# Sparse attention in a four-layer decoder trunk: the compressed branch by four heads of a token tile, its values on 128 rows, and the last queries projected ahead of the last values

## The chip, the core and the metric

The kernel runs on one core of one Trainium2 chip. The core has five engines that take their instructions in order: TensorE (PE in the profile; PEld is its weight load), VectorE (DVE), ScalarE (ACT), GpSimd (POOL) and SyncE (SP), which issues most DMAs. The metric is the device time of one execution in microseconds (us).

## What is computed

A trunk of four layers over 256 tokens of width 1024, all in float32. Each layer is a pre-RMSNorm token mixer and a squared-ReLU MLP of width 4096. The mixers are native sparse attention (layer 0), stick-breaking attention, a Conformer convolution and block-sparse attention. The change touches the mixer of layer 0 only:

```python
q = _apply_rope(_rms_norm(q), cos, sin)                 # 8 heads of 128
kc, ks, kw = [rope(rms_norm(k))]                        # 2 groups, 4 heads each
kc = einsum('bnlgd,lde->bnge', kc[:, cidx] + pos, w_cmp[0])   # blocks of 32, stride 16
vc = einsum('bnlgd,lde->bnge', vc[:, cidx] + pos, w_cmp[1])
p_c = _masked_softmax(q . kc * scale, cmp_end <= t);  o_c = p_c @ vc
p_s = _masked_softmax(q . k_selected * scale, causal); o_s = p_s @ v_selected
p_w = _masked_softmax(q . kw * scale, window);        o_w = p_w @ vw
o = gate0 * o_c + gate1 * o_s + gate2 * o_w
out = o.reshape(B, S, H * DH) @ w_out
```

With 256 tokens there are four selection blocks and the top 16 are taken, so the selected branch sees every block, and the window of 512 sees every token: both are plain causal attention with their own keys and values. The compressed branch has 15 blocks in each of the two groups, 30 rows, held as 32.

## The kernel before

Activations are held feature-major, in 8 tiles of 128 features by 256 tokens, and tokens in two tiles of 128. A float32 weight is split into a high and a low part in the type fp32r (`piece`, L142: ScalarE casts the high part at L159, VectorE subtracts at L160), and a projection does three fp32r matmuls in place of one (`mm3`, L181 to L186). Attention itself works in plain float32; one such matmul appears in the trace as two records.

`nsa` (L424) is layer 0. `chunk(ci)` (L484) projects one chunk of the input weights for both token tiles, in the order of `NSA_CHUNKS`: compressed keys and values; selected and window keys; queries of heads 0 to 3; values of group 0 with the gates; values of group 1 with the query of head 4; queries of heads 5 to 7. `queries` (L468) takes the norm of a head (sum of squares, then a power on GpSimd, L385), its negated copy `nrq` (L471) and the rope on VectorE (L392, L393, L402). `transpose_to` (L455) queues four transposes and their copy in the list `waiting`, which `flush` or the next projection empties.

`compress(kv)` (L542) forms the block sums: 64 matmuls of 32 columns (L553) from two DMAs of 1 MB, a copy `part` (L559), and one matmul with 0/1 entries (`quarters`) that adds the parts: for keys it gives 32 columns, copied behind the 256 keys in `kcat`; for values 32 rows, `vcmp`.

`scores(h, t)` (L569) is one head and token tile (a unit): the masks are added by matmuls of the identity with the mask (L579, L581, L594, L597), then the query meets the keys of the selected, window and compressed branch (L583 for the first tile, L599 and L604 for the second). VectorE takes three maxima and the negative scaled maximum `nm` (L611), ScalarE three exponentials with their sums (L615), VectorE the reciprocals times the gates (L618 to L620) and the scaling (L622, L623). `mix(h, t, pr)` (L627) transposes the probabilities on TensorE (L633; the 32 compressed columns at L637), copies them, and multiplies by the values (L642; the compressed ones at L643 with 32 rows). `attend` runs a list of units with the mix one unit behind the scores: first the four heads of group 0, later `UNITS` for group 1. `Out` (L231) is the output projection `wo`: 192 matmuls of 256 columns (L212 to L214, tile `acc`).

A scheduler of the framework sets the order of the instructions on each engine when the program is built. It may move work of a later call ahead, so output-projection and query-projection matmuls stand between the steps of attention. PSUM tiles rotate in tags A (2 banks), B (4) and C (2); the names `sc`, `pt`, `pc` are in B, `pp` and `po` in C.

Of the kernel before, what the change touches and what calls it, by code (L numbers as in the profile page):

```python
# [16 lines left out]
P = 128  # L17
# [50 lines left out]
def trunk(ctx: ExitStack, tc: tile.TileContext, A: dict, out: bass.AP):  # L68
# [355 lines left out]
    def nsa(n, first):  # L424
        aT = n.xT
        nxt = start_norm(4)
        with tc.tile_pool(name="nsa", bufs=1) as sp:
# [12 lines left out]
            vcmp = sp.tile([32, DH], F32, name="vcmp")  # L440
            quarters = sp.tile([P, 32], F32, name="quarters")
            oT = act.tile([P, KT, 2, NT, P], F32R, tag="aT", name="oT")
            with tc.tile_pool(name="nsw", bufs=2) as wp:
# [40 lines left out]
                def chunk(ci):  # L484
# [10 lines left out]
                    for t in range(NT):  # L495
# [24 lines left out]
                        elif ci == 5:  # L520
                            queries(t, o[:, :384], 5, 3)
                        else:
                            g = ci - 3
# [6 lines left out]
                            else:  # L530
                                queries(t, o[:, 256:384], 4, 1)
# [10 lines left out]
                def compress(kv):  # L542
# [13 lines left out]
                    if kv == 0:  # L556
                        flush()
# [3 lines left out]
                    if kv == 0:  # L561
                        nc.tensor.matmul(pt[:, :32], lhsT=part, rhs=quarters, start=True, stop=True)
                        for g in range(2):
                            nc.scalar.copy(kcat[:, g, 256:288], pt[:, :32])
                    else:
                        nc.tensor.matmul(pt[:32, :DH], lhsT=quarters, rhs=part, start=True, stop=True)
                        nc.scalar.copy(vcmp, pt[:32, :DH])

                def scores(h, t):  # L569

# [4 lines left out]
                    mx = sm.tile([P, 3], F32, tag="mx", name="mx")  # L575
                    if t == 0:

                        s0 = bank("B", "sc")
                        nc.tensor.matmul(s0[:, 256:288], lhsT=identr, rhs=mk[:, P + 32 * g:][:, :32],  # L579
                                         start=True, stop=False, skip_group_check=True)  # L580
                        nc.tensor.matmul(s0[:, :256], lhsT=identr, rhs=diag2, start=False, stop=False,  # L581
                                         skip_group_check=True)
                        nc.tensor.matmul(s0[:, :288], lhsT=q, rhs=kcat[:, g, :288], start=False, stop=True,  # L583
                                         skip_group_check=True)
                        nc.vector.tensor_reduce(mx[:, 0:2], s0[:, :256].rearrange("p (a b) -> p a b", b=P),
                                                axis=AX.X, op=ALU.max)
                        views = [s0[:, :P], s0[:, P:256], s0[:, 256:288]]
                    else:

                        kb = kcat[:, g]  # L590
                        views = []
                        for br in range(2):
                            s0 = bank("B", f"sc{br}")
                            nc.tensor.matmul(s0[:, P:256], lhsT=identr, rhs=mk[:, :P], start=True, stop=False,  # L594
                                             skip_group_check=True)
                            if br == 0:
                                nc.tensor.matmul(s0[:, 256:288], lhsT=identr, rhs=mk[:, P + 64 + 32 * g:][:, :32],  # L597
                                                 start=False, stop=False, skip_group_check=True)
                                nc.tensor.matmul(s0[:, 256:288], lhsT=q, rhs=kb[:, 256:288], start=False, stop=False,  # L599
                                                 skip_group_check=True)  # L600
                                cmp_view = s0[:, 256:288]
                            rhs = bass.AP(tensor=kb.tensor, offset=kb.offset + br * P,
                                          ap=[kb.ap[0], [288, 2], [1, P]])
                            nc.tensor.matmul(s0[:, :256], lhsT=q, rhs=rhs, start=False, stop=True,  # L604
                                             skip_group_check=True)
                            nc.vector.tensor_reduce(mx[:, br:br + 1], s0[:, :256], axis=AX.X, op=ALU.max)
# [587 lines left out]
```

## Time and profile before

| | us |
|---|---|
| median of 3 runs | 1199.9 (1198.47 to 1200.67) |
| profiled execution, whole | 1198.12 |
| profiled execution, span from the first to the last instruction | 1196.3 |
| TensorE busy in the span | 1174.8 (98%) |
| VectorE, ScalarE, GpSimd busy | 779.8, 623.4, 34.7 |
| layer 0's mixer, from the first matmul to the first of the MLP | 7.6 to 147.2 |

TensorE is busy nearly all the time. Its records overlap, because a matmul starts before the one ahead of it has ended, so a busy time is not what a matmul adds. The chain of waits gives each piece from the end of the one before it, and so what it adds.

### The profile page before, as it was taken

What the parts mean: (1) busy time and instruction counts of PE and PEld (TensorE: products, weight loads), DVE (VectorE), ACT (ScalarE), POOL (GpSimd) and SP (SyncE); (2) the same over time, 40 slices, a digit from 0 to 9 for tenths busy, and PEclk for the clock granted to TensorE, in tenths of its full rate; (3) what the DMA queues carried; (4) which work ended last, traced back from release to release, by engine and by line L of the source; (5) the groups of instructions that cost most, each with busy time, mean ns of one, the idle gap of its engine ahead of it and who ended that gap; (6) DMA issues with size and microseconds to landing.
All of it is one profiled execution on the core that took longest, in us unless ns stands there. A gap on an engine that the chain in (4) does not pass through costs nothing.

```text
span 1196.3 us, 17644 instructions
## 1 busy us (share of the span) xinstructions
PE 1174.8 (98%) x7042; PEld 1010.6 (84%) x7042; DVE 779.8 (65%) x1203; ACT 623.4 (52%) x1027; POOL 34.7 (3%) x46
## 2 busy tenths in 40 slices
PE   7999999999999999999999899999999999999998
PEld 5888988888888898888889898888888789888886
DVE  7678676556585477566665578556558876666553
ACT  6477554544465655444553276444447665544441
POOL 1200000000000000000001000000001010000000
PEclk9999999999999999999999999999999999999999
DMA  8553164554454425554546826455354633555440
GB/s 310 189 183 142 71 212 160 196 207 167 185 188 163 154 91 205 207 211 161 196 159 203 257 107 239 148 211 206 146 202 158 222 116 110 208 203 188 172 176 36
DMA packets 35073, 211.23 MB, mean 177 GB/s; under 512 B 4528, under 2 KB 7472, under 8 KB 11440
## 3 DMA queue, kind: packets, MB, share of 16 engines
q1 hardware_dynamic: 30816, 200.99, 46.8%
q0 software_dynamic: 1280, 4.70, 1.4%
q10 hardware_dynamic: 2896, 4.42, 1.1%
q8 instruction: 55, 0.90, 0.3%
q14 instruction: 26, 0.21, 0.1%
HBM read 207.87 MB, written 2.23 MB: 176 GB/s over the span
## 4 chain that ended last, share of the span: by engine, by line
PE 66%; issue 26%; DVE 4%; DMA 2%; ACT 1%; POOL 1%; SPq 0%; ACTq 0%; DVEq 0%; POOLq 0%
PE projT L205 22%; PE dn L186 7%; PE dn L184 7%; PE dn L185 7%; PE ab L873 2%; PE proj L184 2%; PE proj L186 2%; PE proj L185 2%; PE acc L212 2%; PE acc L213 2%; PE acc L214 2%; DVE wl L160 1%; PE po L642 1%; ACT wh L159 1%; PE cv L817 1%
## 5 line engine op out<-in xcount | busy, mean ns | idle before, releaser
L160 DVE TENSOR_TENSOR wl<-raw,wh 128x1024 fp32r<-128x1024 f32 (+2 forms) x376 | 446.0, 1210 | 190.0 <-ACT wh L159 185.3
L159 ACT CAST wh<-raw 128x1024 fp32r<-128x1024 f32 (+2 forms) x376 | 379.7, 1040 | 207.8 <-PE dn L186 111.2
L205 PE MATMUL projT<-xT,wh 128*128 128x512 f32 x1152 | 361.6, 396 | 0.3 <-DVE xT L101 0.3
L205 PEld LDWEIGHTS projT<-xT,wl 128*128 128x128 f32 x1152 | 215.3, 188 | 49.7
L205 PE MATMUL projT<-xT,wl 128*128 128x256 f32 x1152 | 225.8, 278 | 0.0
L184 PE MATMUL dn<-wh,u 128*128 128x512 f32 x512 | 202.7, 396 | 0.0
L186 PE MATMUL dn<-wh,u 128*128 128x512 f32 x512 | 202.0, 395 | 0.0
L185 PE MATMUL dn<-wl,u 128*128 128x512 f32 x512 | 201.4, 393 | 0.0
L205 PEld LDWEIGHTS projT<-xT,wh 128*128 128x128 f32 x1152 | 178.3, 189 | 3.5 <-DVE xT L101 0.5
L186 PEld LDWEIGHTS dn<-wh,u 128*128 128x128 f32 x512 | 96.4, 188 | 22.3
L185 PEld LDWEIGHTS dn<-wl,u 128*128 128x128 f32 x512 | 96.4, 188 | 20.9
L184 PEld LDWEIGHTS dn<-wh,u 128*128 128x128 f32 x512 | 96.5, 188 | 20.3
L184 PE MATMUL proj<-wh,xT 128*128 128x512 f32 (+2 forms) x224 | 87.0, 390 | 8.0 <-ACT wh L159 7.6
L310 ACT COPY b<-projT 128x256 f32<-128x256 f32 x128 | 41.2, 374 | 93.8 <-PE projT L205 93.4
L185 PE MATMUL proj<-wl,xT 128*128 128x512 f32 (+2 forms) x224 | 85.9, 384 | 0.0
L186 PE MATMUL proj<-wh,xT 128*128 128x512 f32 (+2 forms) x224 | 85.7, 383 | 0.0
L311 DVE TENSOR_TENSOR s<-projT,b 128x256 f32<-128x256 f32 x128 | 48.1, 417 | 55.0 <-ACT b L310 55.0
L89 ACT CAST u<-q 128x1024 fp32r<-128x1024 f32 x32 | 33.6, 1049 | 82.8 <-DVE q L313 82.7
L212 PE MATMUL acc<-oT,wh 128*128 128x256 f32 x256 | 73.6, 292 | 0.1
L213 PE MATMUL acc<-oT,wh 128*128 128x256 f32 x256 | 72.9, 286 | 0.0
L214 PE MATMUL acc<-oT,wl 128*128 128x256 f32 x256 | 71.0, 284 | 0.0
L90 DVE TENSOR_TENSOR u<-q,u 128x1024 fp32r<-128x1024 f32 x32 | 39.2, 1226 | 34.6 <-ACT u L89 34.6
(251 smaller groups left out, 1243.5 us busy)
## 6 DMA issues: line engine op xcount, KB each, us to landing
raw<-in_up SPq DMA_DIRECT2D x64, 1024.0 KB, 4.8
raw<-in_down SPq DMA_DIRECT2D x64, 1024.0 KB, 4.9
raw<-in_sb_w SPq DMA_DIRECT2D x12, 1024.0 KB, 4.8
raw<-in_moba_w SPq DMA_DIRECT2D x12, 1024.0 KB, 4.9
raw<-in_conv_w SPq DMA_DIRECT2D x8, 1024.0 KB, 4.9
st<-dr POOLq DMA_DIRECT2D x16, 287.0 KB, 5.2
raw<-in_nsa_w SPq DMA_DIRECT2D x4, 1024.0 KB, 5.2
rawc<-in_nsa_cmp SPq DMA_DIRECT2D x4, 1024.0 KB, 4.8
```

Of the source, the lines that this page charges most:

```text
L90: return a, nc.vector.tensor_sub(lo, src, hi.bitcast(F32))
L159: nc.scalar.copy(wh[:, :w], r)
L160: nc.vector.tensor_sub(wl[:, :w], r, wh[:, :w].bitcast(F32))
L184: nc.tensor.matmul(o, lhsT=aT[:, kt, 0, t, :], rhs=wh, start=first, stop=False)
L185: nc.tensor.matmul(o, lhsT=aT[:, kt, 0, t, :], rhs=wl, start=False, stop=False)
L186: nc.tensor.matmul(o, lhsT=aT[:, kt, 1, t, :], rhs=wh, start=False, stop=last)
L205: nc.tensor.matmul(o[:, :width], lhsT=v[kt][part][:, f * P:(f + 1) * P], rhs=rhs, start=kt == 0 and part == 0, stop=kt == KT - 1 and part ...
L212: nc.tensor.matmul(o, lhsT=wh, rhs=aT[:, kt, 0], start=first, stop=False, skip_group_check=True)
L213: nc.tensor.matmul(o, lhsT=wh, rhs=aT[:, kt, 1], start=False, stop=False, skip_group_check=True)
L214: nc.tensor.matmul(o, lhsT=wl, rhs=aT[:, kt, 0], start=False, stop=last, skip_group_check=True)
L310: nc.scalar.copy(b, o[:, S:])
L311: nc.vector.tensor_add(s[:, f], o[:, :S], b)
```

## The change

The chunk order is turned at its end: chunk 4 is now the queries of heads 4 to 7 (512 columns), chunk 5 the values of group 1 (256 columns, loaded in one piece a half). The compressed branch leaves `scores`: `compressed(g, t)` does the four heads of a group and token tile at once, with one maximum, one exponential and one transpose of 4 x 32 = 128 columns. The transposed probabilities of the four heads then stand on 128 rows, and the compressed values are laid out as four 128-row tiles, each with one head's 32 rows filled and the others zero. `scores` keeps two branches and has one product for both also in the second token tile (512 columns). All transposes are flushed ahead of the first attention call, and the block sums come behind the first and second head's scores. In the output projection, nine of the first sixteen pieces are tied behind the value products of a given unit (`FILL_NSA`).

```diff
+FILL_NSA = (-1,) * 7 + (0, 1, 2, 3, 4, 4, 5, 5, 6)
-UNITS = ((4, 0), (4, 1)) + tuple((h, t) for t in range(2) for h in range(5, 8))
...
-    [("vs", 1), ("vw", 1), ("q", 4)],
-    [("q", 5), ("q", 6), ("q", 7)],
+    [("q", 4), ("q", 5), ("q", 6), ("q", 7)],
+    [("vs", 1), ("vw", 1)],
...
-            for wh, wl in piece(w[:, off + half * n:off + (half + 1) * n], n, 2, before):
-                for k in range(2):
+            parts = 2 if n > 1024 else 1
+            for wh, wl in piece(w[:, off + half * n:off + (half + 1) * n], n, parts, before):
+                for k in range(4 // parts):
...
-                    nc.vector.tensor_scalar(nrq[:, t, h0:h0 + nh], rq[:, t, h0:h0 + nh], -1.0, None, op0=ALU.mult)
                     r = rope(wp, src, nh, G[:, t, 0, 0:1].to_broadcast([P, nh, DH]),
                              G[:, t, 1, 0:1].to_broadcast([P, nh, DH]))
+                    nc.vector.tensor_scalar(nrq[:, t, h0:h0 + nh], rq[:, t, h0:h0 + nh], -1.0, None, op0=ALU.mult)
...
-                        nc.tensor.matmul(pt[:32, :DH], lhsT=quarters, rhs=part, start=True, stop=True)
-                        nc.scalar.copy(vcmp, pt[:32, :DH])
+                        nc.tensor.matmul(pt[:, :DH], lhsT=quarters[:, :P], rhs=part, start=True, stop=True)
+                        nc.vector.tensor_tensor(vcmp, pt[:, None, :DH].to_broadcast([P, 4, DH]),
+                                                quarters[:, P:, None].to_broadcast([P, 4, DH]), op=ALU.mult)
+
+                def compressed(g, t):
+                    hs = slice(4 * g, 4 * g + 4)
+                    sc = bank("B", "scc")
+                    nc.tensor.matmul(sc[:, :P], lhsT=identr,
+                                     rhs=mk[:, None, P + 64 * t + 32 * g:P + 64 * t + 32 * g + 32].to_broadcast([P, 4, 32]),
+                                     start=True, stop=False, skip_group_check=True)
+                    for j in range(4):
+                        nc.tensor.matmul(sc[:, 32 * j:32 * j + 32], lhsT=qT[:, 4 * g + j, t * P:(t + 1) * P],
+                                         rhs=kcat[:, g, 256:288], start=False, stop=j == 3, skip_group_check=True)
+                    z = sc[:, :P].rearrange("p (h n) -> p h n", n=32)
+                    mx = sm.tile([P, 4], F32, tag="mxc", name="mxc")
+                    nc.vector.tensor_reduce(mx, z, axis=AX.X, op=ALU.max)
+                    nc.vector.scalar_tensor_tensor(mx, mx, NEG_SUM, nrq[:, t, hs], op0=ALU.max, op1=ALU.mult)
+                    pr = wp.tile([P, 4, 32], F32, tag="prc", name="prc")
+                    nc.vector.tensor_tensor(pr, z, rq[:, t, hs, None].to_broadcast([P, 4, 32]), op=ALU.mult)
+                    nc.vector.tensor_tensor(pr, pr, mx[:, :, None].to_broadcast([P, 4, 32]), op=ALU.add)
+                    nc.scalar.activation(pr, pr, AF.Exp)
+                    co = sm.tile([P, 4], F32, tag="coc", name="coc")
+                    nc.vector.tensor_reduce(co, pr, axis=AX.X, op=ALU.add)
+                    nc.vector.tensor_scalar(co, co, 1e-30, None, op0=ALU.max)
+                    nc.vector.reciprocal(co, co)
+                    nc.vector.tensor_mul(co, co, gates[:, t, hs, 2])
+                    nc.vector.tensor_tensor(pr, pr, co[:, :, None].to_broadcast([P, 4, 32]), op=ALU.mult)
+                    pt = bank("B", "ptc")
+                    nc.tensor.transpose(pt[:, :P], pr.rearrange("p h n -> p (h n)"), ident)
+                    PTc = wp.tile([P, P], F32, tag="PTc", name="PTc")
+                    nc.scalar.copy(PTc, pt[:, :P])
+                    return PTc
 
                 def scores(h, t):
...
+                    nc.tensor.matmul(z[:, :, t * P:], lhsT=identr, rhs=diag2, start=True, stop=False,
+                                     skip_group_check=True)
+                    keys = kb[:, :256]
+                    if t:
+                        keys = bass.AP(tensor=kb.tensor, offset=kb.offset, ap=[kb.ap[0], [P, 2], [288, 2], [1, P]])
+                    nc.tensor.matmul(s0[:, :2 * w], lhsT=q, rhs=keys, start=False, stop=True, skip_group_check=True)
+                    nm = sm.tile([P, 2], F32, tag="nm", name="nm")
+                    nc.vector.tensor_reduce(nm, z, axis=AX.X, op=ALU.max)
+                    nc.vector.tensor_scalar(nm, nm, nr, None, op0=ALU.mult)
...
-                def mix(h, t, pr):
+                def mix(h, t, pr, PTc):
...
-                    nc.tensor.transpose(po[:32, :P], pr[:, 2 * w:2 * w + 32], ident)
-                    PTc = wp.tile([32, P], F32, tag="PTc", bufs=3, name="PTc")
-                    nc.scalar.copy(PTc, po[:32, :P])
-                    ov = po[:, P:256]
+                    ov = po[:, :P]
+                    nc.tensor.matmul(ov, lhsT=vcmp[:, h % 4], rhs=PTc, start=True, stop=False)
                     for k in range(2 * nb):
-                        nc.tensor.matmul(ov, lhsT=vv[:, k % nb, k // nb, g], rhs=PT[:, k], start=k == 0, stop=False)
-                    nc.tensor.matmul(ov, lhsT=vcmp, rhs=PTc, start=False, stop=True)
+                        mm = nc.tensor.matmul(ov, lhsT=vv[:, k % nb, k // nb, g], rhs=PT[:, k], start=False,
+                                              stop=k == 2 * nb - 1)
...
-                def attend(units, first=None):
+                def attend(g, first=()):
...
+                    units = [(h, t) for t in range(NT) for h in range(4 * g, 4 * g + 4)]
                     for i, (h, t) in enumerate(units):
+                        held.append((h, t, scores(h, t)))
+                        if i < len(first):
                             first[i]()
+                        if i < NT:
+                            PTc.append(compressed(g, i))
                         if i >= LAG:
...
-                compress(0)
-                attend([(h, t) for t in range(NT) for h in range(4)], {1: lambda: compress(1)})
+                flush()
+                attend(0, (lambda: compress(0), lambda: compress(1)))
                 chunk(4)
                 chunk(5)
-                attend(UNITS, {1: lambda: waiting.pop(0)(), 2: flush})
+                flush()
+                last = attend(1)
                 o = Out(oT, A["nsa_wo"], nxt)
-                o.go(range(4), range(4))
+                for kt in range(4):
+                    for m in range(4):
+                        behind = FILL_NSA[4 * kt + m]
+                        if behind < 0:
+                            o.go([kt], [m])
+                        else:
+                            with tc.issue_after(last[behind].ins):
+                                o.go([kt], [m])
```

The scheduler lays the instructions anew. Three places show it; lines of the changed kernel lie further down than those of the kernel before.

On VectorE, the queries of heads 0 to 3 (`m1`, `m2` are the rope's products, `nrq` the negated scale, `ss` the sum of squares; `proj_417` is the first token tile, `proj_418` the second). Before:

```order
L392 TENSOR_TENSOR m1_481<-proj_417,G_91 128x512
L471 TENSOR_SCALAR nrq_100<-rq_99 128x4
L393 TENSOR_TENSOR m2_482<-proj_417,G_91 128x512
L383 TENSOR_REDUCE ss_488<-sq_486 128x4
L402 TENSOR_TENSOR m1_481<-m1_481,m2_482 128x512
L384 TENSOR_SCALAR ss_488<-ss_488,heps_251 128x4
L471 TENSOR_SCALAR nrq_100<-rq_99 128x4
L392 TENSOR_TENSOR m1_493<-proj_418,G_91 128x512
```

With the change:

```order
L393 TENSOR_TENSOR m1_480<-proj_417,G_91 128x512
L394 TENSOR_TENSOR m2_481<-proj_417,G_91 128x512
L475 TENSOR_SCALAR nrq_100<-rq_99 128x4
L384 TENSOR_REDUCE ss_488<-sq_486 128x4
L403 TENSOR_TENSOR m1_480<-m1_480,m2_481 128x512
L385 TENSOR_SCALAR ss_488<-ss_488,heps_251 128x4
L475 TENSOR_SCALAR nrq_100<-rq_99 128x4
L393 TENSOR_TENSOR m1_492<-proj_418,G_91 128x512
```

The negated scale of the first tile moved behind one product of the rope; that of the second tile still stands ahead of its rope.

On TensorE, the start of group 0, behind the projection of chunk 3 (`pt` are query transposes and sums of parts, `sc` and `scc` scores, `pc` block sums, `pp` and `ptc` transposes of probabilities, `po` value products). Before, with the 64 matmuls of the first block sums just ahead of these rows:

```order
L459 MATMUL pt_635<-ident_76,m1_493 128x128 x4
L562 MATMUL pt_643<-quarters_102,part_641 128x32
L579 MATMUL sc_648<-mk_93,identr_85 128x32
L581 MATMUL sc_648<-mk_93,identr_85 128x256
L553 MATMUL pc_667<-rawc_668,kcT_107 32x128 x8
L583 MATMUL sc_648<-kcat_96,qT_95 128x288
L553 MATMUL pc_667<-rawc_668,kcT_107 32x128 x8
L553 MATMUL pc_667<-rawc_686,kcT_107 32x128 x16
L566 MATMUL pt_706<-part_704,quarters_102 32x128
L579 MATMUL sc_710<-mk_93,identr_85 128x32
...
L583 MATMUL sc_710<-kcat_96,qT_95 128x288
L633 MATMUL pp_729<-ident_76,pr_656 128x128 x2
```

With the change:

```order
L461 MATMUL pt_598<-ident_76,m1_492 128x128 x4
L609 MATMUL sc_604<-mk_93,identr_85 128x256
L553 MATMUL pc_617<-rawc_618,kcT_107 32x128 x5
L614 MATMUL sc_604<-kcat_96,qT_95 128x256
L553 MATMUL pc_617<-rawc_618,kcT_107 32x128 x11
L553 MATMUL pc_617<-rawc_636,kcT_107 32x128 x16
L560 MATMUL pt_656<-quarters_102,part_654 128x32
...
L577 MATMUL scc_660<-kcat_96,qT_95 128x32 x4
L634 MATMUL pp_761<-ident_76,pr_610 128x128 x2
L594 MATMUL ptc_679<-ident_76,prc_669 128x128
...
L614 MATMUL sc_683<-kcat_96,qT_95 128x256
L553 MATMUL pc_696<-rawc_697,kcT_107 32x128 x16
```

The block sums moved behind the query transposes and between the scores, and the compressed scores and their transpose stand ahead of the second head's scores and of the second block sums.

On TensorE and VectorE, the start of group 1. Before, on TensorE, from the scores of a first-tile unit to the transposes of the first head:

```order
L583 MATMUL sc_1301<-kcat_96,qT_95 128x288
L213 MATMUL acc0_1551<-oT_103,wh_1527 128x256
L214 MATMUL acc0_1551<-oT_103,wl_1528 128x256
L212 MATMUL acc1_1558<-oT_103,wh_1527 128x256
L213 MATMUL acc1_1558<-oT_103,wh_1527 128x256
L214 MATMUL acc1_1558<-oT_103,wl_1528 128x256
L633 MATMUL pp_1238<-ident_76,pr_1199 128x128 x2
```

With the change, on TensorE:

```order
L461 MATMUL pt_1107<-ident_76,m1_1031 128x128 x4
...
L614 MATMUL sc_1113<-kcat_96,qT_95 128x256
...
L577 MATMUL scc_1126<-kcat_96,qT_95 128x32 x4
L634 MATMUL pp_1185<-ident_76,pr_1119 128x128 x2
L594 MATMUL ptc_1145<-ident_76,prc_1135 128x128
...
L614 MATMUL sc_1149<-kcat_96,qT_95 128x256
...
L577 MATMUL scc_1162<-kcat_96,qT_95 128x32 x4
```

and on VectorE, from the last rope of the queries on (`nm` is the negative scaled maximum of the two branches, `mxc` the compressed one, `wl` a low part of the output weights):

```order
L394 TENSOR_TENSOR m2_1032<-proj_964,G_91 128x512
L475 TENSOR_SCALAR nrq_100<-rq_99 128x4
L160 TENSOR_TENSOR wl_1394<-raw_1387,wh_1393 128x1024
L403 TENSOR_TENSOR m1_1031<-m1_1031,m2_1032 128x512
L160 TENSOR_TENSOR wl_1400<-raw_1397,wh_1399 128x1024
L160 TENSOR_TENSOR wl_1404<-raw_1397,wh_1403 128x1024
L616 TENSOR_REDUCE nm_1116<-sc_1113 128x2
L581 TENSOR_REDUCE mxc_1132<-scc_1126 128x4
L617 TENSOR_SCALAR nm_1116<-nm_1116,nrq_100 128x2
```

The transposes of the first head moved directly behind its compressed scores, with no output-projection matmul between, and on VectorE the compressed maximum stands between the first head's maximum and its product with the scale.

## Rows read from the trace of the kernel before

**Rows 1.** The page: its first line, and the weight split's group.

```profile
span 1196.3 us, 17644 instructions
...
L160 DVE TENSOR_TENSOR wl<-raw,wh 128x1024 fp32r<-128x1024 f32 (+2 forms) x376 | 446.0, 1210 | 190.0 <-ACT wh L159 185.3
```

**Rows 2.** Waits, TensorE, 52 to 150 us: who waits for whom, total, times, longest.

```profile
PE pt L566 <- ACT part L559: 0.6, 1, 0.6
PE pc L553 <- DMA rawc<-in_nsa_cmp: 0.3, 1, 0.3
PE pt L459 <- DVE mx L609: 0.2, 1, 0.2
PE pt L459 <- DVE ss L384: 0.2, 1, 0.2
PE sc L599 <- ACT qT L464: 0.2, 1, 0.2
```

**Rows 3.** Stretches: length, busy time and count of each engine, clock, DMA.

```profile
99.06:133.00 33.94, 33.01 (x221) 27.71 (x221) 23.67 (x91) 21.51 (x79) 1.71 (x2) 1.00 0.23 88
```

**Rows 4.** The chain, 52 to 70 us: start, time it adds, what.

```profile
52.29 1.89 PE pc L553 x64
54.18 1.52 PE pt L459 x12
...
57.45 0.42 DVE mx L585
...
58.00 0.24 DVE nm L611
...
61.57 0.21 PE sc L581
61.78 0.48 PE sc L583 x2
...
62.98 0.44 PE po L642 x4
63.43 0.41 PE po L643 x2
63.84 0.26 PE sc L594
64.10 0.07 PE sc L597
64.17 0.24 PE sc L599 x2
64.40 0.51 PE sc L604 x2
64.92 0.06 PE sc L594
64.97 0.48 PE sc L604 x2
...
66.44 0.11 PE po L637
```

**Rows 5.** Timeline of VectorE: start, duration, line, operation, tiles, idle time before.

```profile
52.84 0.17 DVE L471 TENSOR_SCALAR nrq<-rq 128x4 f32<-128x4 f32 x1 [1.12 <-POOL rq L385]
...
54.23 0.69 DVE L402 TENSOR_TENSOR m<-m,m 128x512 f32<-128x512 f32 x1
...
59.93 0.18 DVE L619 RECIPROCAL co<-co 128x3 f32<-128x3 f32 x1
...
60.34 0.42 DVE L622 TENSOR_TENSOR pr<-pr,co 128x256 f32<-128x256 f32 x1
...
84.09 0.28 DVE L392 TENSOR_TENSOR m<-proj,G 128x128 f32<-128x128 f32 x1
```

**Rows 6.** Timeline of ScalarE: the first and the third exponential of a unit.

```profile
58.35 0.46 ACT L615 ACTIVATE pr<-sc,nm,rq 128x128 f32<-128x128 f32 x1 [1.74 <-DVE nm L611]
...
59.24 0.37 ACT L615 ACTIVATE pr<-sc,nm,rq 128x32 f32<-128x32 f32 x1
```

**Rows 7.** Stretches at the start and in the convolution.

```profile
7.60:12.80 5.20, 5.16 (x11) 3.63 (x12) 4.51 (x8) 4.26 (x10) 0.00 (x0) 1.00 1.05 427
12.80:18.00 5.20, 5.20 (x23) 4.27 (x22) 5.20 (x10) 4.74 (x8) 0.00 (x0) 1.00 0.88 309
680.00:692.00 12.00, 8.89 (x214) 7.69 (x215) 5.05 (x14) 2.48 (x7) 1.03 (x3) 1.00 0.46 140
```

More of the change, by code (lines that the diff above doesn't have):

```diff
@@ L439, in nsa @@
             nrq = sp.tile([P, NT, NH], F32, name="nrq")
-            vcmp = sp.tile([32, DH], F32, name="vcmp")
-            quarters = sp.tile([P, 32], F32, name="quarters")
+            vcmp = sp.tile([P, 4, DH], F32, name="vcmp")
+            quarters = sp.tile([P, P + 4], F32, name="quarters")
             oT = act.tile([P, KT, 2, NT, P], F32R, tag="aT", name="oT")
@@ L519, in chunk @@
                             queries(t, o, 0, 4)
-                        elif ci == 5:
-                            queries(t, o[:, :384], 5, 3)
+                        elif ci == 4:
+                            queries(t, o, 4, 4)
                         else:
-                            g = ci - 3
+                            g = ci // 5
                             nc.scalar.mul(vv[:, t, :, g], o[:, :256].rearrange("p (a b) -> p a b", b=P), rx[t])
@@ L561, in compress @@
                     if kv == 0:
-                        nc.tensor.matmul(pt[:, :32], lhsT=part, rhs=quarters, start=True, stop=True)
+                        nc.tensor.matmul(pt[:, :32], lhsT=part, rhs=quarters[:, :32], start=True, stop=True)
                         for g in range(2):
@@ L574, in scores @@
                     r_, nr = rq[:, t, h:h + 1], nrq[:, t, h:h + 1]
[L575 to L606, printed above, removed]
-                            views.append(s0[:, :256])
-                        views.append(cmp_view)
@@ L609, in scores @@
-                    nc.vector.tensor_reduce(mx[:, 2:3], views[2], axis=AX.X, op=ALU.max)
-                    nm = sm.tile([P, 3], F32, tag="nm", name="nm")
-                    nc.vector.tensor_scalar(nm, mx, NEG_SUM, nr, op0=ALU.max, op1=ALU.mult)
-                    pr = wp.tile([P, 544], F32, tag="pr", bufs=4, name="pr")
-                    sums = sm.tile([P, 3], F32, tag="sums", name="sums")
-                    for br, (a, b) in enumerate(((0, w), (w, 2 * w), (2 * w, 2 * w + 32))):
-                        nc.scalar.activation(pr[:, a:b], views[br], AF.Exp, bias=nm[:, br:br + 1], scale=r_,
-                                             accum_out=sums[:, br:br + 1])
@@ L617, in scores @@
-                    co = sm.tile([P, 3], F32, tag="co", name="co")
-                    nc.vector.tensor_scalar(co, sums, 1e-30, None, op0=ALU.max)
-                    nc.vector.reciprocal(co, co)
-                    nc.vector.tensor_mul(co, co, gates[:, t, h])
-                    v = pr[:, :2 * w].rearrange("p (a b) -> p a b", a=2)
-                    nc.vector.tensor_tensor(v, v, co[:, 0:2, None].to_broadcast([P, 2, w]), op=ALU.mult)
-                    nc.vector.tensor_scalar(pr[:, 2 * w:2 * w + 32], pr[:, 2 * w:2 * w + 32], co[:, 2:3], None,
-                                            op0=ALU.mult)
+                    kb = kcat[:, g]
@@ new lines, in scores @@
+                    nm = sm.tile([P, 2], F32, tag="nm", name="nm")
+                    nc.vector.tensor_reduce(nm, z, axis=AX.X, op=ALU.max)
+                    nc.vector.tensor_scalar(nm, nm, nr, None, op0=ALU.mult)
+                    pr = wp.tile([P, 512], F32, tag="pr", bufs=4, name="pr")
+                    p = pr[:, :2 * w].rearrange("p (b k) -> p b k", b=2)
+                    co = sm.tile([P, 2], F32, tag="sums", name="sums")
+                    for br in range(2):
+                        nc.scalar.activation(p[:, br], z[:, br], AF.Exp, bias=nm[:, br:br + 1], scale=r_,
+                                             accum_out=co[:, br:br + 1])
```

26 lines of the change are left out of this document (13 added, 13 removed).

## The prediction

> **What bounds the kernel now.** First comes the page: the span is 1196.3 us [rows 1] in an execution of 1198.12 us, so 1.8 us lie around it; the median of the runs shown is 1199.9 us, 1.8 us above that execution. Then who waits: TensorE, in the first layer behind its first transposed weights, waits five times for 1.5 us in all, the longest 0.6 us for the evicted block sums [rows 2], and between 99 and 133 us it is busy for 33.0 of 33.9 us [rows 3]. So this layer is bound by TensorE's own sequence: what leaves the sequence is gained, and a new hole in it is lost, because the MLP behind it has no free time on TensorE in which to catch up. Last the chain of waits from 52 to 70 us [rows 4], where each piece of TensorE work stands with the time that it adds: these are the prices below, since the busy time of one matmul overlaps the next. The short VectorE and ScalarE steps of a softmax are priced from their timelines [rows 5, 6].
>
> **TensorE's own work.** The value product of the compressed branch with 32 rows costs 0.41 us for its pair of records; four records with 128 rows cost 0.44, a pair 0.22 [rows 4]. Sixteen of them: 16 x 0.19 = 3.0 us less. A transpose of 32 columns adds 0.11 us, one of 128 columns 1.52/12 = 0.13 [rows 4]; sixteen become four: 1.8 - 0.5 = 1.3 us less. The scores of the second token tile are now 0.26 + 0.07 + 0.24 + 0.51 + 0.06 + 0.48 = 1.62 us [rows 4]; then they are one mask of 0.21 and one product of 512 columns, which the trace does not have here: twice the 256-column one, 0.96, is my value; it cannot be below 0.48, and 2 x 0.51 is the upper end. 1.62 - 1.17 = 0.45, times eight units: 3.6 us less (3.1 to 7.4). The scores of the first tile go from 0.02 + 0.21 + 0.48 to 0.21 + 0.48: nothing. New are sixteen 32-column products at 0.24 us and four masks at some 0.1 [rows 4]: 4.3 us more. The projection of the last queries and values keeps its columns, 768 a token tile, in 512 and 256 in place of 384 and 384: nothing. Sum: -3.0 - 1.3 - 3.6 + 4.3 = **-3.6 us**.
>
> A page bears on the first term. The 32-row pair costs 0.41 against 0.22 us [rows 4]. The Trainium skill, "TensorE: Matmul & The Clock Gate", LDWEIGHTS (loading the stationary operand), says that a weight load takes a time set by its columns and that 32 x 128 loads as long as 128 x 128; by it the padding gives nothing, and the time would be 3.0 us above the one that I forecast, 1209.5 us (chance 0.02, within the 0.65 below, since the rows show the price). The Trainium skill, "TensorEngine Tiling (Array Packing)", Key Properties, says that a change of tiling mode drains the engine, and with that the row agrees; the row decides.
>
> **What covers the softmax chains.** TensorE gets its next operand from a chain. Scores of the first tile to transposes of their probabilities: hop 0.03, maximum 0.42, product 0.24, hop 0.11 [rows 4], two exponentials 0.89 from 58.35 to 59.24 [rows 6], reciprocal and gate 0.41, scaling 0.42 [rows 5], hops 0.1: **2.6 us**. The compressed one, new, has nine small VectorE steps (maximum, scale, product, add, sum, clamp, reciprocal, gate, scale) at 0.2 to 0.28 [rows 5], one exponential near 0.3 (bounds 0.37 with 32 columns and 0.46 with 128 plus a sum [rows 6]) and four hops: **2.5 us** (2.2 to 3.1). Before, the first chain is covered by later scores, 64 block-sum matmuls (1.89 us [rows 4]) and, in the second group, by output-projection matmuls. The instruction order printed with the change says what stands there now:
>
> 1. The last four query transposes now follow the projection directly instead of 64 block-sum matmuls. Their rope ends at 54.92 in the trace [rows 5]. The negated scale moved behind the rope for the first tile only; for the second it still stands ahead, behind a 1.12 us wait for GpSimd [rows 5]. The first move brings the rope forward 0.6 us, to 54.3. TensorE is free at 52.29 [rows 4] and has eight transposes, 1.0 us: wait 1.1.
> 2. The first block sums' copy on ScalarE now stands behind two exponentials of the first head: 0.03 + 0.42 + 0.03 + 0.24 + 0.11 + 0.89, copy and hops 0.35, in all 2.1 us after the scores, with 27 block-sum matmuls of 0.03 us (0.9 with the switch) over it: wait 1.1. The second block sums, alike with 32 matmuls: wait 1.0. Copying the compressed keys adds 0.25.
> 3. The first compressed transpose stands right behind the first head's two transposes (0.22): 2.5 - 0.22 = wait 2.3. Scores and block sums that could fill it come after it.
> 4. The second tile's rope of the last queries: after its projection ScalarE squares (0.6), VectorE reduces, multiplies twice and adds (four times 0.69), adds the epsilon (0.2), waits for GpSimd (0.8) and splits one weight of 1.21 us [rows 1] in between: 5.6 us. TensorE has 35 matmuls of 256 columns, at half of 5.2/23 us [rows 7] 4.0 with a switch: wait 1.4.
> 5. The second group opens with the same pair. On VectorE the compressed maximum, which waits for the compressed scores, stands ahead of the first head's product with the scale: 2.6 us then count from the end of the compressed scores, and the compressed sum (0.2) stands ahead of the scaling, less the maximum that is done: wait 2.7 at the first head's transposes. The compressed transpose comes 0.6 later. The second head repeats it with 1.0 us of value and output matmuls behind its compressed scores: 2.6 - 1.0 is 1.6, of which I take 1.4, since its tail is partly done. The rest of the group: 0.4.
>
> New waits: 1.1 + 1.1 + 1.0 + 0.25 + 2.3 + 1.4 + 2.7 + 0.6 + 1.4 + 0.4 = **12.2 us**. Of the old ones the 1.5 marked go [rows 2] and some short holes that are not marked: -2.0 (0 to -2.5). VectorE and ScalarE do fewer short steps than before, but those lie under TensorE; nothing is taken for them. The weight loads are as many bytes, in fewer, longer pieces; the block-sum buffers are released some 3 us later and the next projection weights with them, but they then have until the query projection, 12 matmuls in, so nothing (0 to 1 us). The padded values cost VectorE one 128x512 product beside the compressed scores: nothing. The output-projection matmuls, tied one by one behind the heads, fill holes of the last four heads; they are as many as before.
>
> **Sum.** 1198.12 - 3.6 + 12.2 - 2.0 = 1204.7 us for the profiled execution; 1.8 us more on the scale of the median: **1206.5 us**. What a measurement of this kernel can tell from no change is about 0.2%, 2.4 us, so faster is below 1197.5 and slower above 1202.3.
>
> **Rivals.** *The chains are covered after all*: the new waits are no longer than the old. What is left is TensorE's work, 1199.9 - 3.6 = 1196.3 us, faster. For it: before, TensorE hardly waits although the chains are as long. Against: there other work stands in the printed order between scores and transposes; here the next instruction is the waiting one, and TensorE takes its matmuls in order. It decides if waits 3 and 5 together stay under 2 us in place of 7. Chance 0.08.
>
> *Half the waits*: chains overlap better than I add them, or the compressed steps run at 0.1 us each: 1199.9 - 3.6 + 6.1 - 2.0 = 1200.4 us, no change. Chance 0.17.
>
> *The pace of TensorE falls in the holes*: between 7.6 and 12.8 us, behind the wait at the start, 11 matmuls run where the next 5.2 us hold 23, though the granted clock reads 1.00, the level of 2.4 GHz, in both [rows 7]. The opening of the second group leaves TensorE idle for some 6 of 13 us. Should one such stretch follow, 5.2 us do half their work: 2.6 us more, 1209.1 us, slower. Against: between 680 and 692 us it is idle for 3.1 of 12 us and the granted clock stays 1.00 [rows 7]. The Trainium skill, "TensorE: Matmul & The Clock Gate", Part 1, has a clock gate that falls to half after idleness; by that rule this rival would come about, and the second of these rows does not bear it out for single holes below 3 us. Chance 0.10.
>
> **How the numbers follow.** My sum has chance 0.65 (1203 to 1208.5: price of the wide product, old waits, a third of the new ones), the slower rival 0.10, half the waits 0.17, covered 0.08. The range from 1199.0 to 1210.0 leaves out the covered case and the far end of the slower one. Faster 0.08, same 0.17, slower 0.75.
>
> **What would show it.** In the profile after: TensorE's list of waits grows from 1.5 to some 12 us, led by transposes that wait for VectorE, two of them over 2 us; the value product with compressed probabilities costs about 0.22 a pair; the first MLP matmuls come some 7 us later. I am wrong if the printed order's neighbours show no idle time between them, or if the first transposes of the second group start within 1 us of the compressed scores' end.

## The result and the profile after

The changed kernel takes **1208.7 us** (median of 4 runs, 1207.9 to 1209.8), the kernel before 1200.2 beside it: ratio 1.0079, 95% interval 1.0067 to 1.0091. It is slower, as forecast (1206.5), and by more than a measurement of this kernel can miss. The profiled execution took 1207.92 us.

The page after; the second line is the granted clock in 40 slices, in tenths.

```profile
span 1206.1 us, 17496 instructions
...
PEclk9988999999999999999999999999999999999999
```

The span of the profiled execution grew by 9.8 us [rows 1], where the medians differ by 8.5. In the slices 3 and 4 (60 to 121 us) the clock line shows 8, which is new. The first matmul of the first MLP starts at 156.75 us; before it started at 147.19. So 9.6 of the 9.8 us arise ahead of it, in the first layer; these are what the rest of this document accounts for.

Waits of TensorE after, 52 to 165 us: who waits for whom, total, times, longest.

```profile
PE pp L634 <- DVE coc L589: 3.5, 2, 2.9
PE ptc L594 <- DVE prc L592: 2.4, 1, 2.4
PE pt L461 <- DVE gt L530: 1.3, 1, 1.3
PE pt L461 <- DVE m L403: 1.2, 1, 1.2
PE po L639 <- ACT PT L636: 0.5, 2, 0.3
PE pt L564 <- ACT part L557: 0.4, 1, 0.4
PE pt L560 <- ACT part L557: 0.4, 1, 0.4
```

That is 9.7 us in place of 1.5 [rows 2], led by transposes behind VectorE. These 8.2 us are the first part of the loss. The second is seen in the stretches of the same trace (length, busy time and count of TensorE, granted clock, DMA):

```profile
60.82:63.24 2.42, 0.00 (x0) 0.67 1.00 423
63.30:68.20 4.90, 4.90 (x68) 0.50 0.35 105
...
109.91:112.83 2.92, 0.00 (x0) 1.00 0.99 362
112.90:123.00 10.10, 9.46 (x37) 0.50 0.12 51
123.10:133.00 9.90, 9.46 (x54) 1.00 0.00 1
```

Twice, in or right behind the hole in front of the first transposes, the granted clock falls from 1.00 to 0.50, from the level of 2.4 GHz to that of 1.2 GHz, and stays there for 4.9 and 10.1 us of nearly unbroken work. The timeline of TensorE shows what that does to a matmul:

```profile
63.24 0.45 PE L594 MATMUL ptc<-ident,prc 128*128 128x128 f32 x1 [2.42 <-DVE prc L592]
...
64.69 3.64 PE L553 MATMUL pc<-rawc,kcT 128*32 128x128 f32 x64
...
68.96 0.30 PE L573 MATMUL scc<-mk,identr 128*128 128x128 f32 x1
...
69.99 0.49 PE L639 MATMUL po<-PTc,vcmp 128*128 128x128 f32 x2
...
112.83 0.66 PE L634 MATMUL pp<-ident,pr 128*128 128x128 f32 x2 [2.92 <-DVE coc L589]
...
125.60 1.02 PE L614 MATMUL sc<-kcat,qT 128*128 128x512 f32 x2
...
126.57 1.02 PE L614 MATMUL sc<-kcat,qT 128*128 128x512 f32 x2
```

The 64 records of the second block sums take 3.64 us; at a granted clock of 1.00 64 such records took 1.89 [rows 4]. Behind 69 and 123 us the clock is back. There the compressed scores of four heads take 69.99 - 68.96 = 1.03 us, and mask and 512-column product of a second-tile unit 126.57 - 125.60 = 0.97.

### The profile page after: what moved, and what is told of

It reads as the page before. It is cut to its first block, busy times and chain, and to the rows that moved or that the text cites. A ratio compares the mean times of both kernels' runs of the same rounds, so it can differ in the third digit from the quotient of the medians.

```text
span 1206.1 us, 17496 instructions
## 1 busy us (share of the span) xinstructions
PE 1175.5 (97%) x7010; PEld 1009.5 (84%) x7010; DVE 778.7 (65%) x1170; ACT 615.8 (51%) x980; POOL 33.7 (3%) x44
## 4 chain that ended last, share of the span: by engine, by line
PE 65%; issue 26%; DVE 5%; ACT 2%; DMA 2%; POOL 1%; SPq 0%; ACTq 0%; DVEq 0%; POOLq 0%
PE projT L206 22%; PE dn L185 7%; PE dn L187 7%; PE dn L186 7%; PE ab L887 2%; PE proj L185 2%; PE proj L186 2%; PE proj L187 2%; PE acc L213 2%; PE acc L214 2%; PE acc L215 2%; DVE wl L160 1%; PE po L641 1%; ACT pr L622 1%; ACT wh L159 1%
## 5 line engine op out<-in xcount | busy, mean ns | idle before, releaser
L160 DVE TENSOR_TENSOR wl<-raw,wh 128x1024 fp32r<-128x1024 f32 (+1 forms) x374 | 446.0, 1216 | 190.8 <-ACT wh L159 186.1
L159 ACT CAST wh<-raw 128x1024 fp32r<-128x1024 f32 (+1 forms) x374 | 379.2, 1045 | 208.9 <-PE dn L187 111.2
```

The lines of the kernel that those rows point to most:

```text
L159: nc.scalar.copy(wh[:, :w], r)
L160: nc.vector.tensor_sub(wl[:, :w], r, wh[:, :w].bitcast(F32))
```

## Experiments: the holes and the clock

**Theory**: the loss is two things, the holes in which TensorE waits for softmax chains, and the clock that falls at the two openings; the change's own TensorE work saves time. **Rivals**: the clock is only seen and costs nothing; or the chain by four heads always costs a hole, wherever it is put. Beside the experiments the kernel before had medians of 1198.8 to 1199.6, so distances to it are told too; the changed kernel's is 8.5.

**Holes filled with work that nobody needs.** Nothing moves, the waiting instruction only finds TensorE busy:

```diff
+    with tc.issue_after(tps[0].ins if g == 0 else scc.ins):
+        for i in range(18 + 4 * g):
+            filler = nc.tensor.matmul(pt[:, 256:512], lhsT=identr, rhs=diag2, start=True,
+                                      stop=True, skip_group_check=True)
 ...                                    # the waiting transposes keep their place, behind the fillers
```

> The changed kernel with 40 matmuls that compute nothing needed (the causal mask as a product with the unit matrix, 256 columns) written into the unused half of the bank of the compressed transpose: 18 in the hole in front of the first compressed transpose (2.42 us in the changed kernel), 22 in the hole in front of the first transposes of the last four heads (2.92 us). All other instructions of TensorE keep their order. Theory A, the fallen clock is a price on top of the waits: the granted clock stays 1.00, the half-pace stretches 61.67 to 68.22 and 112.86 to 123.06 vanish, which gives back 5.0/2 and 9.2/2 us = 7.1, less about 1.5 of waits that the slow work had covered: 1203.1 us. Theory B, only the waits cost: fillers change nothing, 1208.7 us. If the clock falls all the same: above 1208.7.

Measured: 1204.6 us (1.0052 of before, 1.0035 to 1.0068), 5.9 above the kernel before in place of 8.5; the first MLP matmul starts at 151.95, 4.8 us earlier. The profiled execution is a long one of its kernel (1207.2 us): it loses 4.1 us again behind the first layer, 2.6 of them in the convolution (last section), so the start of the MLP is the better measure. Stretches of this run (columns as above):

```profile
60.70:63.20 2.50, 2.50 (x22) 1.00 1.01 426
63.30:68.20 4.90, 4.40 (x82) 1.00 0.64 211
109.00:112.80 3.80, 3.24 (x26) 1.00 0.86 321
112.90:123.00 10.10, 8.38 (x46) 1.00 0.00 0
```

and its longest wait:

```profile
PE pp L658 <- DVE coc L597: 1.5, 1, 1.5
```

The clock holds at 1.00 through both openings, and useless work makes the first layer faster: the clock is a cost of its own, and the rival that it costs nothing falls. Its full price is larger than 4.8: the wait at the second head's transposes is now 1.5 us where the slow work had left 0.54, and fillers (2.37 us for 18, 2.85 for 22 in the timeline) and listed waits (6.6) together are 11.8 us against 9.7, so 2.1 had been covered. That gives 4.8 + 2.1 = 6.9 us, near the (4.90 + 9.46)/2 = 7.2 that halving the pace of the busy time in the two stretches would give.

**First scores of the last four heads ahead of the last values' projection.** One opening mended with the kernel's own work:

```diff
                 chunk(4)
-                chunk(5)
-                flush()
-                last = attend(1)
+                waiting.pop(0)()
+                last = attend(1, then=lambda: (chunk(5), flush()))   # "then" runs behind compressed(1, 0)
```

> The changed kernel with the first scores and the first compressed scores of the last four heads issued ahead of the projection of the last values, so that the softmax chains run beside its 48 matmuls (5.8 us). Theory A: the waits of 2.92 and most of 1.20 + 0.54 at the opening of the last four heads go, and with them the second fall of the clock (4.6 less 1.5): 1208.7 - 3.5 - 3.1 = 1202.1 us; the granted clock from 106 to 130 is 1.00. Rival, the chains of the second tile come late instead: 1206 or more, with a new wait in front of the compressed transpose of the second tile.

Measured: 1201.2 us (1.0013, 1.0003 to 1.0022), 2.4 above the kernel before; first MLP matmul 149.07, 7.7 us earlier. Two stretches of TensorE (columns as above), and its two longest waits:

```profile
112.00:118.00 6.00, 4.58 (x24) 1.00 0.47 171
118.00:124.00 6.00, 5.59 (x35) 1.00 0.00 1
```

```profile
PE ptc L594 <- DVE prc L592: 2.4, 1, 2.4
...
PE pp L634 <- DVE coc L589: 1.2, 1, 1.2
```

The 2.92 wait is gone, 1.2 is left at the second head, and the clock stays up. The opening of the last four heads was worth most of the loss.

**Output projection in that hole.** Seven pieces (21 matmuls) tied behind the compressed scores in place of the later heads:

```diff
-FILL_NSA = (-1,) * 7 + (0, 1, 2, 3, 4, 4, 5, 5, 6)
+FILL_NSA = (-1,) * 7 + (8,) * 7 + (1, 2)      # 8: behind the compressed scores of (1, 0)
```

> The changed kernel with seven pieces of the output projection (21 matmuls, 2.5 us at full pace) placed directly behind the first compressed scores of the last four heads, ahead of the first transposes there, where they fill the hole of 2.92; they are missing between the later units. Theory A: the hole falls to about 0.4, the second fall of the clock goes: 1208.7 - 2.5 - 3.1 = 1203.1 us. Rival, the pieces are missed later and the holes move there: 1207 to 1208.7.

Measured: 1205.0 us (1.0045, 1.0032 to 1.0058), 5.4 above the kernel before. Theory and rival are both partly right: the hole falls to 0.35, but the next one grows from 0.54 to 1.87, and the clock falls after it all the same (TensorE's timeline, and a stretch of 1 us):

```profile
117.72 0.41 PE L637 MATMUL pp<-ident,pr 128*128 128x128 f32 x2 [1.87 <-DVE coc L592]
```

```profile
119.00:120.00 1.00, 1.00 (x6) 0.57 0.00 0
```

**Block sums moved back, and the values' sums forward.** The other opening:

```diff
+                    if kv == 0:
+                        flush()
...
-                flush()
-                attend(0, (lambda: compress(0), lambda: compress(1)))
+                compress(0)
+                attend(0, (lambda: compress(1),))
```

> The changed kernel with the block sums of the keys again ahead of the last transposes of the first four heads' queries (as in the kernel before) and those of the values behind the first scores, ahead of the first compressed scores. Theory A (the first four heads' holes cost their length and, by the clock, as much again): the waits of 1.33 and 0.38 are covered, the block weights of the values arrive some 4 us earlier so that their 32 products stand ahead of the compressed chain, the 2.42 hole fills with projections, the first fall of the clock goes (2.5): 1208.7 - 6.6 = 1202.1 us. Rival, the compressed chain only moves and TensorE waits for it elsewhere with the clock falling there: within 1.5 us of 1208.7.

Measured: 1207.5 us (1.0061, 1.0045 to 1.0076), 8.7 above the kernel before and so no gain: a miss by 5 us, and the number of the rival. Its reason is another, though. The waits of 1.33, 0.38 and 2.42 are gone, but with the sums out of the way TensorE meets the next projection's weights, which aren't split yet; and the clock still falls, though no hole there is longer than 0.93 us. The opening of the last four heads still has its hole here. Waits from 52 to 80 us, and stretches of 1 us:

```profile
PE proj L186 <- DVE wl L160: 0.9, 1, 0.9
PE proj L185 <- ACT wh L159: 0.7, 1, 0.7
```

```profile
64.00:65.00 1.00, 1.00 (x5) 0.85 0.33 119
65.00:66.00 1.00, 1.00 (x4) 0.50 0.54 70
```

The executions of this one kernel differ: three with a mean granted clock of 0.991 took 1208.2 to 1208.6 us, two with 0.995 took 1204.5 and 1204.8 (one with 0.993: 1206.7). The same program, 3.8 us apart.

**Both openings**, first as the scheduler orders it:

```diff
-                flush()
-                attend(0, (lambda: compress(0), lambda: compress(1)))
+                compress(0)                                   # with the flush inside, as above
+                attend(0, then=lambda: compress(1))           # behind compressed(0, 0)
 ...                                                           # and chunk(5) as in the run above
```

> The changed kernel with both openings mended: the keys' block sums ahead of the last query transposes as before, the values' block sums behind the first compressed scores (so that they run while VectorE and ScalarE work on these), and the first scores of the last four heads ahead of the projection of the last values. Theory A (holes and the clock's falls at the two openings are the loss, all else of the change saves): 1201.2 (the run with the second opening mended) less 1.3 + 0.4 of waits, less some 2 of the 2.4 in front of the first compressed transpose, less 2.5 of half pace: 1195.0 us, below the kernel before at 1198.8. Rival, the first opening can't be mended because the projection's weights come late instead, as in the run with only the block sums moved: 1200 to 1202.

Measured: 1204.4 us (1.0037, 1.0024 to 1.005). A miss: the printed order put the first transposes ahead of the values' sums again (2.64 us), and at the last four heads the first transposes and the compressed one came late by 1.26 and 1.65. The clock fell to 0.50 behind both. Waits, 50 to 165 us:

```profile
PE pp L636 <- DVE coc L591: 3.2, 2, 2.6
PE ptc L596 <- DVE prc L594: 2.1, 2, 1.6
```

Then with the order forced: transposes behind the values' sums, the last projection behind the compressed scores.

```diff
+                    with tc.issue_after(sums[1].ins):
+                        ...                       # the transposes in mix and of the compressed tile
+                                with tc.issue_after(asked[-1].ins):
+                                    then()        # chunk(5)
```

> As combo2, with three orders of TensorE forced that were left to the scheduler there: the values' 32 block-sum products stand between the first compressed scores and the first transposes (in combo2 they stood behind these and waited with them, 2.64 us), and the projection of the last values stands behind the first compressed scores of the last four heads (in combo2 half of it stood ahead, and their chain came late by 1.3 and 1.65 us). Theory A (the loss is holes and falls of the clock at the two openings, and the change's own work saves some 5.7 us): the granted clock stays 1.00 from 52 to 150, waits of TensorE there below 3 us: 1198.8 - 5.7 + 1.5 = 1194.6 us. Rival, the compressed chain by four heads always costs a hole somewhere: 1199 or more.

Measured: **1197.7 us**, ratio 0.9987 (0.9978 to 0.9997): the change, with its openings filled, is level with the kernel before or a little faster (1.4 us). But not the 1194.6 of the theory. Two of the waits, and stretches, of the profiled execution, which at 1200.7 us was the longest of 11:

```profile
PE pp L644 <- DVE coc L595: 2.1, 2, 1.5
...
PE proj L186 <- DVE wl L160: 1.3, 1, 1.3
```

```profile
108.00:109.00 1.00, 0.07 (x1) 0.69 0.00 0
109.00:110.00 1.00, 1.00 (x4) 0.50 0.00 0
...
115.00:116.00 1.00, 1.00 (x5) 0.89 0.00 0
```

5.1 us of waits are left, and in this execution one fall of the clock in this layer, within a hole of 1.51 us behind the compressed chain; another follows in the convolution (last section). So the rival that the chain costs a hole wherever it is put is not excluded: no order tried here is without one. Over the 11 executions time follows the mean granted clock: 0.995 in 1200.6 and 1200.7 us, 0.996 in 1199.1 and 1199.3, 0.997 to 1.0 in 1195.8 to 1198.0.

## Experiments: the change's own work

**Padding alone, in the kernel before.**

```diff
-            vcmp = sp.tile([32, DH], F32, name="vcmp")
+            vcmp = sp.tile([P, DH], F32, name="vcmp")             # zero but for 32 rows
-                    PTc = wp.tile([32, P], F32, tag="PTc", bufs=3, name="PTc")
-                    nc.scalar.copy(PTc, po[:32, :P])
+                    PTc = PTcs[0]                                 # one of three, zero but for 32 rows
+                    PTcs.append(PTcs.pop(0))
+                    nc.scalar.copy(PTc[:32], po[:32, :P])
```

> The kernel before with one part alone: the compressed values and the compressed weights of each head padded with zeros to 128 rows, so that the last product of a unit reads 128 rows and not 32 (written zero once, ahead of the layer's work). By the prediction's term (0.41 to 0.22 us a pair of records, 16 pairs): 1200.2 - 3.0 = 1197.2 us. Rival, a product of 32 rows costs no more than one of 128 and the 0.41 was a matter of its neighbours: 1200.2 us. The copies keep 32 rows, so ScalarE does the same work.

Measured: **1195.1 us**, ratio 0.9958 (0.9945 to 0.9972); the first MLP matmul starts at 142.65, 4.5 us earlier. The same unit in the timeline of the kernel before

```profile
67.33 0.61 PE L642 MATMUL po<-PT,vv 128*128 128x128 f32 x4
67.87 0.48 PE L643 MATMUL po<-PTc,vcmp 32*128 32x128 f32 x2
68.28 0.44 PE L633 MATMUL pp<-ident,pr 128*128 128x128 f32 x2
```

and here:

```profile
67.26 0.61 PE L647 MATMUL po<-PT,vv 128*128 128x128 f32 x4
67.71 0.39 PE L648 MATMUL po<-PTc,vcmp 128*128 128x128 f32 x2
67.93 0.38 PE L637 MATMUL pp<-ident,pr 128*128 128x128 f32 x2
```

The pair costs 0.41 with 32 rows and 0.22 with 128. And the four records ahead of it end earlier too, 0.45 in place of 0.54: the price lies ahead of the pair too, 0.28 in all, times 16 = 4.5 us, what the first MLP matmul shows.

**Padding undone, in the changed kernel.**

```diff
-   nc.tensor.matmul(ov, lhsT=vcmp[:, h % 4], rhs=PTc, start=True, stop=False)
+   j = 32 * (h % 4)
+   nc.tensor.matmul(ov, lhsT=vcmp[j:j + 32, h % 4], rhs=PTc[j:j + 32], start=True, stop=False)
```

> The changed kernel with the value product of the compressed branch over 32 rows again (the 32 rows of that head in the transposed tile and in the values), all else as it is. Theory A, a 32-row product among 128-row ones costs its own 0.41 instead of 0.22 and slows its neighbour too (4.5 us over 16 products, as the run with padding alone gave at the first MLP matmul): 1212.4 us, somewhat less if part of it falls into waits. By the prediction's term: 1208.7 + 3.0 = 1211.7. Rival, the rows make no difference: 1208.7.

Measured: 1211.0 us (ratio 1.0100, 1.0086 to 1.0114), 2.3 above the changed kernel; the first MLP matmul starts at 160.25, 3.5 us later. The rival that rows don't count falls a second time. Part of the price lies in waits here: the 0.54 in front of the second head's transposes is gone.

**Padding and one wide product for the second tile, per head, in the kernel before.**

```diff
-    for br in range(2):
-        s0 = bank("B", f"sc{br}")
-        ...                                   # mask of 128 columns, product of 256, maximum, per branch
+    s0 = bank("B", "sc0")
+    z = s0[:, :512].rearrange("p (b k) -> p b k", b=2)
+    nc.tensor.matmul(z[:, :, P:], lhsT=identr, rhs=diag2, ...)
+    nc.tensor.matmul(s0[:, :512], lhsT=q, rhs=rhs, ...)
+    s1 = bank("B", "sc1")                     # mask and product of the 32 compressed columns
+    nc.vector.tensor_reduce(mx[:, 0:2], z, axis=AX.X, op=ALU.max)
```

> The kernel before with padding, and with window and selected keys of a second-tile unit scored by one 512-column product into one bank, the compressed 32 columns into a bank of their own, per head as before. In the changed kernel mask and 512-column product of such a unit take 0.97 us start to start; before, the unit took 1.62 of which 0.33 were the compressed columns: 0.32 saved, 8 units: 1195.05 - 2.6 = 1192.5 us. By the prediction's 1.17 for mask and product: 1194.1. Rival, the wider tile makes the exponentials and so the transposes late: 1195 or more with new waits.

Measured: **1192.5 us**, ratio 0.994 (0.9927 to 0.9954), the fastest here. That it is just the 1192.5 expected is luck: the first MLP matmul starts at 141.67, only 1.0 us ahead of padding alone and not 2.6, because two waits came with the product (50 to 165 us). The other 1.5 of the 2.5 us between the two profiled executions lie in the convolution, where padding alone met a fallen clock (64 records in 3.43 us) and this run did not (1.96):

```profile
PE po L636 <- DVE oT L90: 0.9, 1, 0.9
PE pt L463 <- DVE m L402: 0.6, 1, 0.6
```

These two parts of the change are worth 7 us by the medians and 5.5 at the first MLP matmul; the rest of it, the compressed branch by four heads and the order around it, spent them again and 8.5 more. No run shows a gain from the batching itself: with its openings filled it is 1.4 us below the kernel before, and these two parts without it are 7.1 below.

## Why the prediction was right, and where it was not

The direction and its main reason held: transposes behind softmax chains with nothing in front of them. The size came out near (1206.5 against 1208.7) by luck: two misses of opposite sign nearly cancelled, work and waits 5.3 us less than forecast and a clock that cost 6.9 more. Up to the first MLP matmul, in us:

| term | forecast | measured |
|---|---|---|
| value product with 128 rows | -3.0 | -4.5 (padding alone) |
| second tile's scores | -3.6 | (1.62 - 0.97) x 8 = -5.2 |
| compressed scores | +4.3 | 1.03 x 4 = +4.1 |
| transposes | -1.3 | not measured alone |
| waits, new less old | +10.2 | 9.7 - 1.5 = +8.2 |
| granted clock | 0 | +6.9 (filled holes) |
| sum | +6.6 | +9.6 in all |

The measured terms with the forecast -1.3 for the transposes add up to 8.2; 1.4 us are not assigned.

- **TensorE's work** was mis-sized twice, on the same side. The 32-row product also holds up the records ahead of it (0.54 in place of 0.45), which the chain's prices [rows 4] did not show. And the 512-column product was put at twice the 256-column one, 0.96 behind a mask of 0.21; mask and product together are 0.97.
- **Waits 1, 3 and 4** were right: 1.33 for 1.1, 2.42 for 2.3, 1.20 for 1.4. In the first, the rope came forward by less than the 0.6 us taken: it ends at 54.69, before at 54.92.
- **Wait 2** failed: 0.38 and 0.39 in place of 1.1 and 1.0. The step took 27 block-sum matmuls at the price of a record; each matmul is two records, so they lay over the copy for 1.73 us and not 0.9. (The block sums of keys or of values are 32 matmuls, 64 records; where 64 matmuls are spoken of ahead of the result, records are meant.)

```profile
56.70 1.73 PE L553 MATMUL pc<-rawc,kcT 128*32 128x128 f32 x54
```

- **Wait 5** was 2.92 for 2.7; the compressed transpose followed without the 0.6; the second head waited 0.54 for 1.4, but only since the slow work before it stretched: with the clock held it is 1.5.
- **The rival on TensorE's pace**, given 0.10, is what happened on top of the forecast case, not in its place, and at both openings. The step that failed is the reason against it: that the clock stays at 1.00 from 680 to 692 us with 3.1 us idle [rows 7] was taken to clear single holes below 3 us. It doesn't: the longest hole in it is 2.33 us, and in the changed kernel half pace followed one of 2.42. The rival's price was also too small: two stretches, 6.9 us, in place of one with 2.6.
- **The rule of the Trainium skill** on loads set by columns ("TensorE: Matmul & The Clock Gate", LDWEIGHTS) agrees with the loads themselves, 182 ns with 32 rows and 192 with 128 (the kernel before, and padding alone). What was drawn from it, that padding gains nothing, is not so: padding alone gained 3.7 us by the medians, undoing it lost 2.3. The clock gate of the Trainium skill ("TensorE: Matmul & The Clock Gate", Part 1), which falls to half after idleness, agrees with both openings (1.00 to 0.50); the last section has holes behind which the clock did not fall.

```profile
L643 PEld LDWEIGHTS po<-PTc,vcmp x32: 181/182/184, 63.4 to 132.1; 32*128 32x128 f32 x32
L648 PEld LDWEIGHTS po<-PTc,vcmp x32: 192/192/192, 63.4 to 127.6; 128*128 128x128 f32 x32
```

- The later release of the block-sum buffers, taken as nothing, costs nothing in the changed kernel; where the sums are moved, the split of those weights becomes the wait (0.9 and 1.3 us).

## What to carry to other kernels

Price a hole in a dense TensorE sequence at its length and, apart from that, at what a fallen clock would cost behind it; filling it even with useless matmuls tells the two apart in one run. Before a group of small softmaxes is batched, look at what stands between the batch's scores and its transposes, and put a projection or a sum there; here that order made the difference between 8.5 us lost and 1.4 gained. Where a few rows enter a product between full ones, try padding them with zeros: here it was worth 3.7 us, more than any of the batched kernels gained.

## What was not expected of the hardware

- The granted clock is no fixed function of the program. Executions of one kernel with filled openings lie between 0.995 and 1.0 and, with that, between 1195.8 and 1200.7 us; with the block sums moved, 1204.5 and 1208.6 us.
- It fell in the changed kernel within a hole of 2.42 us and at the end of one of 2.92, within one of 1.51 us with the openings filled, and with the block sums moved only after work had resumed, with no hole above 0.93 us ahead. From 680 to 692 us of the kernel before it stayed up with 3.1 us idle [rows 7], 2.33 of them in one hole, and in the kernel with fillers it stayed up behind a hole of 1.51. What sets these apart stays open.
- The same is seen in the convolution of a later layer, which the change doesn't touch. There the same 64 records stand behind a wait for a DMA, and run at full or at half pace; the length of the wait alone does not tell which. In order: the changed kernel, the output projection in the hole, both openings with the order forced, and the fillers.

```profile
697.46 1.95 PE L831 MATMUL cv<-st,taps 128*32 128x128 f32 x64 [2.25 <-DMA st<-dr]
693.87 1.95 PE L834 MATMUL cv<-st,taps 128*32 128x128 f32 x64 [3.02 <-DMA st<-dr]
688.61 3.62 PE L847 MATMUL cv<-st,taps 128*32 128x128 f32 x64 [2.69 <-DMA st<-dr]
693.70 3.55 PE L860 MATMUL cv<-st,taps 128*32 128x128 f32 x64 [4.82 <-DMA st<-dr]
```

  So part of what executions of one kernel differ by arises there, and a time compared over the whole kernel carries it; the start of the first MLP matmul does not.
- Padding a product from 32 to 128 rows speeds up its neighbour: 0.09 of the 0.28 us a unit lie in the records ahead of it.
